# Making the beta-scaled values of the delta rule ahead of its solves

## The chip, the cores and the metric

The kernel runs on one core of one Trainium2 chip. The metric is the device time of one execution in microseconds. Three runs of the kernel before gave 1041.5, 1041.88 and 1042.18 us; the median is 1041.88 us. A further execution was recorded by the profiler, and every duration below comes from it.

## What is computed

One residual encoder block works on 512 tokens of width 1024: a SwiGLU feed-forward half step, a token mixer, and a second feed-forward half step, all in f32. The mixer adds two groups of heads, a gated delta rule (4 heads of width 128) and a latent attention (4 heads). The change lies in the delta rule. Cut to what matters, for each chunk:

```python
A = jnp.where(strict, beta[..., :, None] * kk * decay, 0.0)
M = A + jnp.eye(CHUNK)
rhs = jnp.concatenate([v * beta[..., None], k * (beta * jnp.exp(G))[..., None]], axis=-1)
W = lax.linalg.triangular_solve(M, rhs, left_side=True, lower=True, unit_diagonal=True)
u, wk = W[..., :GDN_DV], W[..., GDN_DV:]
...
v_new = u_c - wk_c @ state
o_c = qd_c @ state + qk_c @ v_new
state = state * gl_c + kd_c.T @ v_new
```

The product `v * beta` (in the kernel with the norm of k folded into the factor) is the subject. It needs the convolved and activated values and one factor per token and head. It does not need the inverse of M.

## The kernel before, in words

The kernel treats the 512 tokens as four blocks of 128. Activations lie with features on the partitions; dense products are split into three matmuls each (lines 453, 454 and 455, high and low parts) so that f32 accuracy comes out.

**Order of emission.** The code is a set of generators. `dense_units` (line 1271) emits one 128-column unit of a projection as four steps of two k-tiles, six matmuls each, and behind each step it advances three side queues by a rate: `chain` (keys, the matrix A, its inverse, then the solves), `deltas` (the products of q and k, the norms of q) and `att` (the attention). The mixer runs the units of k, of q, of v and of z (the output gate) in this order, four units each, which is 16 steps each. During z the rates are 1 for `chain`, 0.75 for `deltas` and 2.67 for `att`. `deltas` runs its generators one after the other: `delta_qk` (4 blocks of work) and `delta_q` (4 and one more), which go in during v and the first steps of z. Behind z a loop (line 2059) advances `chain` by two, the attention by four, and when the attention is through, `out_attended` (line 2108), the attention's part of the output projection. Behind that loop `recur` (line 1702) carries the state from block to block, with its matmuls in the order in which they are written.

**Queues.** The emitted order is not quite the order of the engines' queues. The tile framework fills each engine's queue by a list schedule: of the instructions that its model holds ready, the one emitted first goes first. [...]

**The solve.** `inverse(p)` builds the inverse U of block p through eight stages (lines 1598 to 1668), all four blocks interleaved. `solve(p)` (line 1670), two blocks interleaved, does in its first stage: four transposes of the values into a PSUM bank (`token_major`, line 1489), the product `vb` on VectorE from that bank (helper `mul`, line 1269), for p > 0 the product `kbg`, for p < 3 the product `kd` (both line 1269, from SBUF). In its second stage eight matmul records multiply U with `vb` (line 1689), and ScalarE copies the result `uu` (line 1691). In its third stage, for p > 0, eight records multiply `kbg` with U (line 1698), copied to `w` (line 1700). `recur(0)` begins with line 1730, which needs `uu` and `kd` of block 0.

**Buffers.** Most SBUF tiles of 128x512 f32 come from one pool of 56 slots (`slot`, line 113). The convolved tiles of k, q and v come from another, of 12 (`slot(late=True)`, lines 1477 and 951). PSUM has two pools: three banks for dense products (`pa`) and five for all else (`pb`).

Of the kernel before, what the change touches and what calls it, by code (L numbers as in the profile page):

```python
# [23 lines left out]
NB = NT // P  # L24
# [68 lines left out]
class Block:  # L93
# [1576 lines left out]
    def solve(self, p, vT):  # L1670

        nc = self.nc
        h4 = lambda x: x.rearrange("p (h d) -> p h d", h=4)
        hs = lambda h: slice(h * P, (h + 1) * P)
        c4 = slice(4 * p, 4 * p + 4)
        u = self.inv[p]
        vb = self.slot(s="vb")
        self.mul(h4(vb), h4(self.token_major(vT, p)), self.bc(self.kn[:, c4], 4))
        kt = self.kt[p]
        if p > 0:  # L1680
            kbg = self.slot(s="kbg")
            self.mul(h4(kbg), h4(kt), self.bc(self.eG[:, c4], 4))
        if p < NB - 1:
            self.kd[p] = self.slot(s="kd")
            self.mul(h4(self.kd[p]), h4(kt), self.bc(self.kcd[:, c4], 4))
        yield
        pu = self.aux()
        for h in range(4):
            nc.tensor.matmul(pu[:, hs(h)], u[:, hs(h)], vb[:, hs(h)], start=True, stop=True)
        self.us[p] = self.slot(s="uu")  # L1690
        nc.scalar.copy(self.us[p], pu)
        if p == 0:
            self.wk[0] = True
            return
        yield
        pw = self.aux()
        for h in range(4):
            nc.tensor.matmul(pw[:, hs(h)], kbg[:, hs(h)], u[:, hs(h)], start=True, stop=True)
        self.wk[p] = self.slot(s="w")
        nc.scalar.copy(self.wk[p], pw)  # L1700

    def recur(self, p):

# [264 lines left out]
    def mixer(self, norms):  # L1968
# [21 lines left out]
                self.table(t, t, AF.Silu, after=after)  # L1990

        self.inv = [None] * NB
        self.kd, self.us, self.o, self.wk = ([None] * NB for _ in range(4))
        self.S = None

        def prepared():
# [33 lines left out]
        def solving():  # L2030
            solves = Side(wide=2)
            solves.add(*(self.solve(p, vT) for p in range(NB)))
            while solves.open or solves.todo:
                solves.step(2)
                yield

        chain.add(solving())
        self.dense_units(4, Rates(sides, (1, 0.75, 2.67)), 1, z_done)
        w1 = self.ins["ffn2_w_in"][0]
        self.firsts, early = [], Side()  # L2040
# [164 lines left out]
```

## Time and profile before

| | us |
|---|---|
| median of the runs | 1041.88 |
| lowest and highest run | 1041.5 and 1042.18 |
| the profiled execution | 1041.97 |
| its span in the trace | 1040.3 |
| outside the span | 1.67 |
| VectorE busy | 753.8 |
| ScalarE busy | 498.5 |

In the rows below, a line L1689 is line 1689 of the kernel. PE is the matmul engine (TensorE), PEld its weight loads, DVE is VectorE, ACT is ScalarE, POOL is GpSimd, SP issues the DMAs. A timeline row gives start, duration, engine, line, operation, the tile written and the tiles read (without numbers), shapes and count; in brackets the idle time of that engine just before, and what ended it. Durations of pipelined instructions overlap, so the step from one start to the next is what an instruction costs its engine. A window row gives, for a stretch of the span, its length and the busy time and count of each engine.

### The profile page before, as it was taken

The page shows a single profiled execution, that of the slowest core. Times are in us where ns is not written, and L with a number is a line of the kernel's source. Part 1 is how long each engine was busy: PE and PEld are TensorE (multiplying, and loading weights), DVE is VectorE, ACT ScalarE, POOL GpSimd, SP SyncE. Part 2 cuts the span into 40 slices and gives each one's busy share as a digit, 9 for nine tenths or more (in the row PEclk, how much of TensorE's full clock was granted, in tenths as well). Part 3 has the DMA queues.
Part 4 walks back from the last instruction along what each step waited for, and adds up shares of the span by engine and source line. Part 5 has one row for each costly group of instructions (what it writes and reads, how often), then busy time and mean ns, then how long its engine had stood idle before and what let it go on. Part 6 is the DMA issues. An engine that isn't in the chain of part 4 may idle for free.

```text
span 1040.3 us, 16767 instructions
## 1 busy us (share of the span) xinstructions
PE 1023.9 (98%) x6601; PEld 907.6 (87%) x6601; DVE 753.8 (72%) x1327; ACT 498.5 (48%) x910; POOL 29.6 (3%) x74
## 2 busy tenths in 40 slices
PE   7999999999999999999999989999999999999998
PEld 5788899999887898888788779998999999987888
DVE  5789788887787757868697467787788888783221
ACT  4452455556322235478864454364555555632221
POOL 0000000001000000000000001100000000000000
PEclk9999999999999999999999999999999999999999
DMA  9977234334688744211232031103333334383311
GB/s 330 320 230 255 76 89 122 89 116 130 213 297 280 241 126 130 61 42 41 61 83 65 21 87 36 42 24 96 105 92 112 108 97 121 114 271 105 112 48 42
DMA packets 201501, 130.77 MB, mean 126 GB/s; under 512 B 14017, under 2 KB 186062, under 8 KB 201422
## 3 DMA queue, kind: packets, MB, share of 16 engines
q1 hardware_dynamic: 201422, 129.69, 40.7%
q8 instruction: 52, 0.85, 0.3%
q14 instruction: 27, 0.22, 0.1%
HBM read 127.18 MB, written 2.49 MB: 125 GB/s over the span
## 4 chain that ended last, share of the span: by engine, by line
PE 93%; DVE 3%; issue 1%; DMA 1%; POOL 0%; SPq 0%; ACT 0%; POOLq 0%
PE pa L453 17%; PE pa L454 17%; PE pa L455 17%; PE pa L341 17%; PE pb L341 12%; PE pb L1937 1%; PE pb L453 1%; PE pb L455 1%; PE pb L454 1%; PE pb L1917 1%; DMA ar<-in_w_ada 1%; PE pb L1537 1%; PE pb L632 1%; PE pb L1919 0%; PE pb L1489 0%
## 5 line engine op out<-in xcount | busy, mean ns | idle before, releaser
L223 ACT CAST wh<-wr 128x1024 fp32r<-128x1024 f32 (+1 forms) x104 | 103.6, 1002 | 198.7 <-PE pa L454 174.8
L224 DVE TENSOR_TENSOR wl<-wr,wh 128x1024 fp32r<-128x1024 f32 (+1 forms) x104 | 120.5, 1163 | 80.6 <-ACT wh L223 78.6
L453 PE MATMUL pa<-ah,wh 128*128 128x512 f32 (+1 forms) x396 | 146.5, 370 | 0.0
L454 PE MATMUL pa<-al,wh 128*128 128x512 f32 (+1 forms) x396 | 145.0, 366 | 0.0
L455 PE MATMUL pa<-ah,wl 128*128 128x512 f32 (+1 forms) x396 | 144.9, 366 | 0.0
L257 DVE TENSOR_TENSOR wl<-wr,wh 128x1024 fp32r<-128x1024 f32 x90 | 110.0, 1223 | 44.4 <-ACT wh L261 44.4
L453 PE MATMUL pa<-hh,wh 128*128 128x512 f32 (+1 forms) x357 | 136.9, 384 | 0.0
L454 PE MATMUL pa<-hl,wh 128*128 128x512 f32 (+1 forms) x357 | 135.2, 379 | 0.0
L455 PE MATMUL pa<-hh,wl 128*128 128x512 f32 (+1 forms) x357 | 135.2, 379 | 0.0
L261 ACT CAST wh<-wr 128x1024 fp32r<-128x1024 f32 x90 | 91.8, 1052 | 2.7 <-DMA ar<-in_w_ada 1.8
L453 PEld LDWEIGHTS pa<-ah,wh 128*128 128x128 f32 x396 | 74.7, 189 | 14.5 <-ACT wh L223 2.5
L455 PEld LDWEIGHTS pa<-ah,wl 128*128 128x128 f32 x396 | 74.7, 189 | 12.1
L454 PEld LDWEIGHTS pa<-al,wh 128*128 128x128 f32 x396 | 74.7, 189 | 11.7
L453 PEld LDWEIGHTS pa<-hh,wh 128*128 128x128 f32 x357 | 67.3, 189 | 13.3 <-ACT th L1264 0.8
L813 DVE SCALAR_TENSOR_TENSOR aa<-ar,sc,aa 128x512 f32<-128x512 f32 x98 | 73.3, 749 | 6.3 <-DMA ar<-in_w_ada 4.3
L455 PEld LDWEIGHTS pa<-hh,wl 128*128 128x128 f32 x357 | 67.3, 188 | 11.6
L454 PEld LDWEIGHTS pa<-hl,wh 128*128 128x128 f32 x357 | 67.4, 189 | 10.7
L341 PE MATMUL pa<-hh,wh 128*128 128x256 f32 x240 | 68.0, 283 | 0.0
L341 PE MATMUL pa<-th,wh 128*128 128x256 f32 x240 | 67.9, 283 | 0.0
L341 PE MATMUL pa<-tl,wh 128*128 128x256 f32 x240 | 67.9, 283 | 0.0
L341 PE MATMUL pa<-th,wl 128*128 128x256 f32 x240 | 67.9, 283 | 0.0
L341 PE MATMUL pa<-hl,wh 128*128 128x256 f32 x240 | 67.9, 283 | 0.0
(434 smaller groups left out, 2375.3 us busy)
## 6 DMA issues: line engine op xcount, KB each, us to landing
wr<-in_ffn_w_in SPq DMA_DIRECT2D x79, 512.0 KB, 5.0
ar<-in_w_ada SPq DMA_DIRECT2D x104, 256.0 KB, 5.6
wr<-in_ffn_w_out SPq DMA_DIRECT2D x32, 512.0 KB, 4.2
wr<-in_w_in SPq DMA_DIRECT2D x21, 512.0 KB, 4.3
ar<-in_w_ada SPq DMA_DIRECT2D x20, 512.0 KB, 5.9
wr<-in_ffn_w_out SPq DMA_DIRECT2D x16, 384.0 KB, 4.7
wr<-in_w_out SPq DMA_DIRECT2D x8, 512.0 KB, 3.3
wr<-in_ffn_w_in SPq DMA_DIRECT2D x8, 384.0 KB, 5.9
```

The source lines that it names most:

```text
L223: self.nc.scalar.copy(hi, raw)
L224: self.nc.vector.tensor_tensor(out=lo, in0=raw, in1=hi.bitcast(F32), op=ALU.subtract)
L257: sub = lambda out, x, y: nc.vector.tensor_tensor(out=out, in0=x, in1=y, op=ALU.subtract)
L261: nc.scalar.copy(hi[:, :n], raw[:, :n])
L341: nc.tensor.matmul(z, a[:, j, :], b, start=start and j == 0 and i == 0, stop=j == 3 and i == 2, skip_group_check=not start)
L453: mm(out, wh, xh, start=start, stop=False)
L454: mm(out, wh, xl, start=False, stop=False)
L455: mm(out, wl, xh, start=False, stop=stop)
L632: nc.tensor.matmul(pg[32 * q:32 * q + 32, :256], self.sc[:, kc:kc + 1].to_broadcast([P, 32]), a[kc], start=(e == 0), stop=(e == 1), tile_p ...
L813: nc.vector.scalar_tensor_tensor(out=acc, in0=a, scalar=sc, in1=acc, op0=ALU.mult, op1=ALU.add)
L1537: nc.tensor.matmul(pa[:, ps], kh[:, ps], x[:, ps], start=True, stop=True)
L1917: nc.tensor.matmul(ps[:, :n], self.qnT[h][:, ts], self.knT[h][:, :n], start=True, stop=False)
```

## The change

The product `vb` leaves the solve's first stage and gets a function of its own, `values`, which makes the four transposes and the one multiplication of a block. A generator that calls it for the four blocks is put at the end of the `deltas` queue, ahead of the units of z. The solve uses what it finds, and makes the product itself only if it is not there yet. Nothing else is changed; the number of instructions is the same.

```diff
         u = self.inv[p]
-        vb = self.slot(s="vb")
-        self.mul(h4(vb), h4(self.token_major(vT, p)), self.bc(self.kn[:, c4], 4))
-        kt = self.kt[p]
+        if self.vb[p] is None:
+            self.values(p, vT)
+        vb, kt = self.vb[p], self.kt[p]
         if p > 0:
             kbg = self.slot(s="kbg")
             self.mul(h4(kbg), h4(kt), self.bc(self.eG[:, c4], 4))
...
+    def values(self, p, vT):
+        h4 = lambda x: x.rearrange("p (h d) -> p h d", h=4)
+        self.vb[p] = self.slot(s="vb")
+        self.mul(h4(self.vb[p]), h4(self.token_major(vT, p)), self.bc(self.kn[:, 4 * p:4 * p + 4], 4))
...
-        self.kd, self.us, self.o, self.wk = ([None] * NB for _ in range(4))
+        self.kd, self.us, self.o, self.wk, self.vb = ([None] * NB for _ in range(5))
...
         chain.add(solving())
+
+        def ahead():
+            for p in range(4):
+                self.values(p, vT)
+                yield
+
+        deltas.add(ahead())
         self.dense_units(4, Rates(sides, (1, 0.75, 2.67)), 1, z_done)
```

## The prediction

> **What bounds the kernel now.** I read the page's engine shares first, then the chain that ended last, then busy time in stretches around the change, then the engines' timelines inside the stretch that has idle time.
>
> ```profile
> span 1040.3 us, 16767 instructions
> PE 93%; DVE 3%; issue 1%; DMA 1%; POOL 0%; SPq 0%; ACT 0%; POOLq 0%
> ```
>
> Of the chain that ended last 93% is work of the matmul engine; 3% is VectorE's. Moving matmul work changes nothing; only removing time in which PE stands still does. The windows show where it stands still near the change.
>
> ```profile
> 560.00:580.00 20.00, 19.91 (x173) 16.83 (x171) 13.59 (x29) 9.85 (x28) 2.01 (x2) 1.00 0.00 1
> 580.00:600.00 20.00, 20.00 (x170) 14.25 (x169) 9.00 (x24) 9.25 (x22) 0.00 (x0) 1.00 0.14 42
> 600.00:620.00 20.00, 17.23 (x141) 13.91 (x139) 13.05 (x28) 10.91 (x21) 2.02 (x2) 1.00 0.31 92
> 620.00:640.00 20.00, 19.55 (x143) 18.17 (x144) 15.58 (x27) 10.48 (x23) 3.06 (x3) 1.00 0.10 28
> ```
>
> The first number after the length is PE. From 560 to 600 us PE idles 0.09 us; from 600 to 640 it idles 2.77 + 0.45 = 3.22 us, the hole that the change can work on. What PE does there:
>
> ```profile
> 612.89 0.63 PE L1959 MATMUL pb<-ident,on 128*128 128x128 f32 x4 [0.77 <-DVE on L1269]
> 613.45 0.68 PE L1663 MATMUL pb<-U,Y 64*64 64x64 f32 x8
> 614.05 0.55 PE L1489 MATMUL pb<-ident,cv 128*128 128x128 f32 x3
> 614.35 0.48 PE L453 MATMUL pa<-mh,wh 128*128 128x512 f32 x1
> 614.67 0.71 PE L1489 MATMUL pb<-ident,cv 128*128 128x128 f32 x5
> 615.13 0.48 PE L453 MATMUL pa<-mh,wh 128*128 128x512 f32 x1
> ...
> 616.82 0.39 PE L455 MATMUL pa<-mh,wl 128*128 128x512 f32 x1
> 618.87 2.33 PE L1689 MATMUL pb<-vb,U 128*128 128x128 f32 x16 [1.66 <-DVE vb L1269]
> 621.04 0.60 PE L1489 MATMUL pb<-ident,cv 128*128 128x128 f32 x4
> 621.47 1.06 PE L1698 MATMUL pb<-U,kbg 128*128 128x128 f32 x8
> 622.91 1.16 PE L1689 MATMUL pb<-vb,U 128*128 128x128 f32 x8 [0.38 <-DVE vb L1269]
> 623.91 0.60 PE L1489 MATMUL pb<-ident,cv 128*128 128x128 f32 x4
> 624.35 1.06 PE L1698 MATMUL pb<-U,kbg 128*128 128x128 f32 x8
> 625.29 1.16 PE L1689 MATMUL pb<-vb,U 128*128 128x128 f32 x8
> 626.29 1.06 PE L1698 MATMUL pb<-U,kbg 128*128 128x128 f32 x8
> 627.18 1.06 PE L1730 MATMUL pb<-uu,kd 128*128 128x128 f32 x8
> ```
>
> The inverse ends at 614.05. PE transposes the values, does the nine dense matmuls that lie at hand, and then waits 1.66 us for the first `vb` and 0.38 us for the third: **2.04 us for the product that the change moves.** From 614.05 to 627.18 are 13.13 us, in steps from start to start: transposes 0.30 + 0.46 + 0.43 + 0.44 = 1.63; the nine dense matmuls 0.32 + 2.08 = 2.40; L1689 2.17 + 1.00 + 1.00 = 4.17; L1698 1.06 + 0.94 + 0.89 = 2.89; idle 2.04. The first sixteen of L1689 cost 2.17 where two groups of eight cost 2.00 later on: 0.17 us more, a short pause for the second `vb`.
>
> Why is `vb` late? VectorE's queue:
>
> ```profile
> 614.50 0.73 DVE L1965 SCALAR_TENSOR_TENSOR ml<-pb,cwT,mh 128x512 fp32r<-128x512 f32 x1
> 616.12 1.41 DVE L2119 SCALAR_TENSOR_TENSOR xT<-pa,mod,xT 128x512 f32<-128x512 f32 x2 [0.88 <-PE pa L455]
> 617.44 0.68 DVE L1265 TENSOR_TENSOR fl<-fr,fh 128x512 fp32r<-128x512 f32 x1
> 618.04 0.68 DVE L1269 TENSOR_TENSOR vb<-pb,kn 128x512 f32<-128x512 f32 x1
> 618.64 0.68 DVE L1269 TENSOR_TENSOR kd<-ktk,kcd 128x512 f32<-128x512 f32 x1
> 619.24 0.68 DVE L1269 TENSOR_TENSOR vb<-pb,kn 128x512 f32<-128x512 f32 x1
> 619.84 0.68 DVE L1269 TENSOR_TENSOR kbg<-ktk,eG 128x512 f32<-128x512 f32 x1
> ```
>
> The transposes of blocks 0 and 1 were through at about 615.4, but `vb` of block 0 started at 618.04: ahead of it stand two residual additions (L2119), of which the first waited 0.88 us for dense matmuls, and a weight split `fl`. From 616.1 to 623 the path runs through VectorE.
>
> **The change part by part.** *Removed waits.* With all `vb` made long before, L1689 of blocks 0 and 1 needs only U, which is there. The 2.04 us of idle time and the 0.17 us pause go: 2.21 us. *Moved matmul work.* Sixteen transposes, 1.63 us here, go into a stretch in which PE is full. They cost the same there and are missing here: zero. *Moved VectorE work.* Four multiplications at 0.60 us a step (618.04 to 618.64) are 2.4 us. `deltas` advances 0.75 per step of z; the norms of q take its first four steps' share, so the four calls fall on steps 6, 7, 8 and 10 of the 16. The inverse, of eight stages, goes one stage further in four steps, so these are its second and third stage, ahead of the fourth (L1644, still at work at 588.97 below): my estimate is 570 to 590 us. There VectorE has room:
>
> ```profile
> 578.70 0.69 DVE L1922 TENSOR_REDUCE mx<-pb 128x1 f32<-128x512 f32 x1 [3.10 <-PE pb L1920]
> 588.97 0.28 DVE L1644 TENSOR_SCALAR U<-pb 32x128 f32<-32x128 f32 x1 [2.08 <-PE pb L1642]
> ```
>
> Its cover is these gaps (9.00 of 20 us busy). If the cover fails, each multiplication can hold up one link of the inverse or of the attention by 0.60 us, 2.4 us at most, and nothing is to be won there since PE does not idle; I take 0, nearest to the 9.00, and keep 2.4 for the range. Each call holds one of five `pb` banks from its transposes to its multiplication, with the same bounds. ScalarE, POOL and SP get nothing: the moved step issues neither a copy nor a DMA, and passes no queue of theirs.
>
> *What is late next.* The third stage of block 1 (L1698) needs `kbg`, which stays on VectorE, and so does `kd`. After the change PE goes on at 614.05 with two groups of L1689 (2.00) and nine dense matmuls (2.40) and is free at 618.45. When is `kbg` of block 1 ready? `fl` needs the ScalarE cast of its high part:
>
> ```profile
> 616.09 0.60 ACT L1264 CAST fh<-fr 128x512 fp32r<-128x512 f32 x1
> ```
>
> If VectorE takes `fl` at 616.7, one residual addition (0.7), `kd` (0.6) and `kbg` (0.6 and its end), `kbg` is there at 619.3: a new wait of 0.85 us. If it keeps today's order, the two additions now wait for dense matmuls that come 2.00 us later less the 0.76 us of transposes: 617.35 to 618.65, `fl` to 619.25, `kd` to 619.85, `kbg` to 620.5: a new wait of 2.1 us. If `kd` and `kbg` go ahead of the additions, there is none. I take 0.85 and keep 0 and 2.1.
>
> The queue that decides this is seen in the rows: `kd` reads only `ktk` and `kcd`, which the code makes during the units of q, and yet it stood behind `vb` while VectorE idled 0.88 us. [...]
>
> **Sum.** -2.21 + 0 + 0 + 0.85 = -1.36 us, call it -1.3. The profiled execution took 1041.97 us (span 1040.3 and 1.67 outside it, untouched), 0.09 over the median of 1041.88; against the median the forecast is 1040.6 us.
>
> **Rivals.** *First: the wait only changes its name.* VectorE keeps today's order and PE waits 2.1 us for `kbg` at L1698 instead: 1041.8 us. For it: `kbg` and `kd` stand right behind `vb` in the same queue. Against it: without the transposes nothing but `fl` holds them there.
>
> *Second: full relief.* `kd` and `kbg` come early, -2.21 us, and the solve's matmuls, ready earlier, also fill the waits of 0.77 us (row above) and 0.34 us just before:
>
> ```profile
> 610.92 0.50 PE L454 MATMUL pa<-ml,wh 128*128 128x512 f32 x1 [0.34 <-DVE ml L1965]
> ```
>
> That is up to -3.3 us, 1038.6 to 1039.7 us. For it: block 0's inverse is the first to end. Against it: the solve is emitted behind the whole inverse.
>
> *Third, slower: slots.* The values' tiles lie in the pool of 12, but `vb` comes from the common 56. Counting by the code what is held about 575 us: the input of the mixer 16, k by tokens 4, A 4, qk 4, v of the attention 4, U 4, and of the attention's open heads, z and the mixed output about 12; with four to six short-lived tiles that is 51 to 53. Four `vb` held from there to the solve leave one free, or none. Then the attention's or the inverse's next tile waits for another's release. A sign that slots are scarce already:
>
> ```profile
> SPq L131 <- DVE U L1644: 25.6, 1, 25.6
> ```
>
> SP stood 25.6 us before a load of the next feed-forward's weights into such slots, until the inverse was well on. The price: one link of attention slips behind the end of z's dense matmuls, where little filler is left. Its part off PE is
>
> ```profile
> 580.57 0.15 DVE L1924 TENSOR_TENSOR mx<-mx,rqn 128x1 f32<-128x1 f32 x1
> ...
> 581.84 0.78 ACT L196 ACTIVATE pr<-pb,mx,rqn 128x512 f32<-128x512 f32 x1
> ...
> 587.45 0.59 ACT L1933 COPY pT<-pb 128x512 f32<-128x512 f32 x1 [0.17 <-PE pb L1931]
> ```
>
> with the 0.69 of the reduction above 2.2 us; two of them exposed, one for each of the last two heads, are 4.4 us, and less the 1.3 won +3.1: 1045.0 us. It decides from the point where fewer than four slots are free while z's units run. Against it: no row of 560 to 600 us shows PE, VectorE or ScalarE standing for a slot today, and z's last unit frees the 16 input tiles one by one.
>
> *Fourth: it does not do what it says*, because the multiplications stay queued where they were: 1041.9 us. Little speaks for it, since nothing in the step waits for the inverse.
>
> **How the numbers follow.** A measurement of this kernel tells about 0.2% from no change, 2.1 us: faster is below 1039.8, slower above 1044.0. Forecast 0.35 (1040.0 to 1041.4), first rival 0.10, second 0.26, third 0.26, fourth 0.03. Faster is the second rival, 0.26; slower the third, 0.26; within 0.2% the rest, 0.48. The queues are laid out anew by any change, so the outer cases keep weight. The range goes from the far end of the second, 1038.5, to 1045.2, just beyond the third's price; the unknown 2.4 us of the z stretch on top of the forecast (1043.0) lies inside. The likeliest case alone spans 1040.0 to 1041.4.
>
> **What would show it.** Right: four `vb` multiplications and 16 transposes between 570 and 595 us; no wait for `vb` at L1689; PE's next wait in the solve names `kbg` at L1698 and is near 0.85 us; PE idle from 600 to 640 falls from 3.22 to about 2. First rival: that wait near 2.1. Third: new idle time of PE between 590 and 615 with attention or inverse as the releaser, and ScalarE or VectorE rows there that wait for a tile's earlier reader. The forecast is wrong if PE idles newly in 560 to 600 us, or if the order of the attention's and inverse's matmuls is another.

## The result, and the profile after

The changed kernel took 1040.34 us (median of 21 runs) where the kernel before took 1042.71 us (median of 21 runs). The ratio on record, with its interval, is not quite that of the medians (0.9977): it is **0.9981, 95% interval 0.9975 to 0.9987**, or 2.0 us faster, between 1.35 and 2.6 us. That is just inside the 0.2% that the prediction set as the limit of "no change", and the interval leaves zero out. The forecast was a gain of 1.3 us, just below the interval: taken off the 1041.88 us of the forecast, 2.0 us give 1039.9, between the forecast's likeliest case (1040.0 to 1041.4) and the second rival's (1038.6 to 1039.7). Which of the two it was, the traces tell.

Line numbers behind the solve are 5 higher in the new kernel (L1730 is now L1735, L1715 is L1720, L1964 was L1959), and those behind the new generator 12 higher (L2131 was L2119). First the page of the kernel after, the head and the chain by engine (its trace has one record fewer than the one before, though the diff takes no instruction away):

```profile
span 1038.6 us, 16766 instructions
...
PE 93%; DVE 3%; issue 2%; DMA 1%; SPq 0%; POOL 0%; ACT 0%; POOLq 0%
```

The bound is the same, PE. Then the four windows of the kernel after (length, then busy time of PE, PEld, DVE, ACT, POOL):

```profile
560.00:580.00 20.00, 19.91 (x168) 17.49 (x167) 13.97 (x29) 9.01 (x26) 2.02 (x2) 1.00 0.01 4
580.00:600.00 20.00, 20.00 (x174) 14.29 (x173) 9.66 (x23) 9.03 (x23) 0.00 (x0) 1.00 0.09 27
600.00:620.00 20.00, 18.89 (x158) 15.23 (x156) 12.12 (x28) 10.77 (x22) 2.02 (x2) 1.00 0.36 107
620.00:640.00 20.00, 19.32 (x140) 17.81 (x139) 16.11 (x31) 12.09 (x27) 3.09 (x3) 1.00 0.09 27
```

PE idles 0.09 us between 560 and 600, as before: the moved work made no new hole. Between 600 and 640 it idles 1.11 + 0.68 = 1.79 us instead of 3.22. The PE timeline of the kernel after shows what is left:

```profile
613.01 0.50 PE L454 MATMUL pa<-ml,wh 128*128 128x512 f32 x1 [0.34 <-DVE ml L1970]
...
614.98 0.63 PE L1964 MATMUL pb<-ident,on 128*128 128x128 f32 x4 [0.77 <-DVE on L1269]
615.54 0.67 PE L1663 MATMUL pb<-U,Y 64*64 64x64 f32 x8
616.14 0.71 PE L1689 MATMUL pb<-vb,U 128*128 128x128 f32 x4
616.61 0.47 PE L453 MATMUL pa<-mh,wh 128*128 128x512 f32 x1
...
619.88 0.40 PE L455 MATMUL pa<-mh,wl 128*128 128x512 f32 x1
620.96 1.13 PE L1698 MATMUL pb<-U,kbg 128*128 128x128 f32 x8 [0.68 <-DVE kbg L1269]
621.92 1.06 PE L1689 MATMUL pb<-vb,U 128*128 128x128 f32 x8
...
625.51 1.06 PE L1735 MATMUL pb<-uu,kd 128*128 128x128 f32 x8
```

No L1689 waits for `vb` any more; the waits of 1.66 and 0.38 us are gone. L1689 starts at 616.14, as soon as the inverse (L1663) is through. In their place stands one wait, 0.68 us, at L1698 for `kbg`. The waits of 0.34 and 0.77 us ahead of it are as they were. VectorE's timeline in the kernel after says why `kbg` is late:

```profile
618.26 0.75 DVE L2131 SCALAR_TENSOR_TENSOR xT<-pa,mod,xT 128x512 f32<-128x512 f32 x1 [0.93 <-PE pa L455]
618.92 0.68 DVE L1265 TENSOR_TENSOR fl<-fr,fh 128x512 fp32r<-128x512 f32 x1
619.52 0.69 DVE L1269 TENSOR_TENSOR kd<-ktk,kcd 128x512 f32<-128x512 f32 x1
620.12 0.68 DVE L1269 TENSOR_TENSOR kbg<-ktk,eG 128x512 f32<-128x512 f32 x1
```

One residual addition, the weight split `fl`, one `kd`, then `kbg`: PE waited out the end of this row of four. The second of the two additions, which stood ahead of `fl` in the kernel before, now comes behind `kbg` (at 621.33). The moved work itself stands where it was looked for; the row of the tile `vb` groups the four multiplications, and the first and the last of the four groups of transposes in the PE timeline are

```profile
L1269 DVE TENSOR_TENSOR vb<-pb,kn x4: 651/664/685, 571.5 to 583.0; 128x512 f32<-128x512 f32 x4
```

```profile
569.89 0.60 PE L1489 MATMUL pb<-ident,cv 128*128 128x128 f32 x4
...
579.01 0.60 PE L1489 MATMUL pb<-ident,cv 128*128 128x128 f32 x4
```

**How far the trace agrees with the runs.** Two executions differ in their first 50 us (the last section shows it), so spans are compared here from a common anchor, the first matmul of the inverse:

```profile
550.17 1.16 PE L1618 MATMUL pb<-t,at 128*128 128x128 f32 x8
```

in the kernel before, and in the kernel after

```profile
550.33 1.16 PE L1618 MATMUL pb<-t,at 128*128 128x128 f32 x8
```

From there to the end of the span are 1040.3 - 550.17 = 490.1 us before and 1038.6 - 550.33 = 488.3 after: 1.8 us less, inside the interval of the runs. All of it is won by the end of the solve: from the anchor to the first matmul of the recurrence are 627.18 - 550.17 = 77.01 before and 625.51 - 550.33 = 75.18 after, 1.83 less. From there to the end both take 413.1 us.

### The profile page after: what moved, and what is told of

It reads as the page before. It is cut to its first block, busy times and chain, and to the rows that moved or that the text cites. A ratio compares the mean times of both kernels' runs of the same rounds, so it can differ in the third digit from the quotient of the medians.

```text
span 1038.6 us, 16766 instructions
## 1 busy us (share of the span) xinstructions
PE 1022.6 (98%) x6601; PEld 906.7 (87%) x6601; DVE 752.9 (72%) x1327; ACT 498.3 (48%) x910; POOL 29.7 (3%) x74
## 4 chain that ended last, share of the span: by engine, by line
PE 93%; DVE 3%; issue 2%; DMA 1%; SPq 0%; POOL 0%; ACT 0%; POOLq 0%
PE pa L453 17%; PE pa L454 17%; PE pa L455 17%; PE pa L341 17%; PE pb L341 12%; PE pb L1942 1%; PE pb L453 1%; PE pb L455 1%; PE pb L454 1%; PE pb L1922 1%; DMA ar<-in_w_ada 1%; PE pb L1537 1%; PE pb L632 1%; PE pb L1489 0%; PE pb L1924 0%
## 5 line engine op out<-in xcount | busy, mean ns | idle before, releaser
L341 PE MATMUL pa<-hh,wl 128*128 128x256 f32 x240 | 67.9, 283 | 0.0
```

Of the source, the lines that this page charges most:

```text
L341: nc.tensor.matmul(z, a[:, j, :], b, start=start and j == 0 and i == 0, stop=j == 3 and i == 2, skip_group_check=not start)
```

## The experiments

The theory on trial is the prediction's: PE stood still for `vb`, that wait is gone, and `kbg` with `kd` ahead of it is late next. Its rivals: the gain comes from less VectorE work in the stretch of the solve, whatever is taken out of it; or the held tiles make slots scarce and eat part of the gain. Every kernel is the changed one with an edit. The column "to the end" is the one worked out above, for the profiled execution. From the first matmul of the recurrence to the end it holds 413.1 or 413.2 us in every kernel (e4: 412.7), so what tells the kernels apart lies ahead of that. Five of them (the change, e6, e7, e9, e10) need 9.36 or 9.37 us from the end of the inverse to the recurrence, and still differ by up to 0.4 us in the column; a difference of that size in the column alone is not worth explaining.

| kernel | ratio to before, 95% | to the end |
|---|---|---|
| before | 1 | 490.1 |
| the change | 0.9981 (0.9975 to 0.9987) | 488.3 |
| e1, two `vb` ahead | 0.9983 (0.9972 to 0.9993) | 488.8 |
| e2, `kd` behind `kbg` | 0.9977 (0.9967 to 0.9986) | 487.8 |
| e3, `kbg` and `kd` ahead too | 0.9980 (0.9971 to 0.9989) | 487.8 |
| e4, made right ahead of the solve | 0.9990 (0.9980 to 1.0000) | 488.8 |
| e5, as e3, solve joined to the inverse | 0.9988 (0.9975 to 1.0000) | 487.9 |
| e6, dummy tiles, freed at once | 0.9980 (0.9971 to 0.9990) | 488.3 |
| e7, each `vb` made three times | 0.9986 (0.9975 to 0.9998) | 488.1 |
| e8, only `kbg` and `kd` ahead | 0.9993 (0.9984 to 1.0001) | 489.5 |
| e9, eight slots held | 0.9982 (0.9972 to 0.9992) | 487.9 |
| e10, twelve slots held | 0.9978 (0.9968 to 0.9988) | 488.2 |

Between two of these kernels the intervals of the runs mostly overlap; what tells them apart are the waits in their traces.

### e1: two of the four products ahead

```diff
-            for p in range(4):
+            for p in range(2):
                 self.values(p, vT)
```

> Only blocks 0 and 1 are made ahead; 2 and 3 stay inside their solves. Theory of waits (the gain is PE's idle time for vb in the solve, given back in part as a new wait for kbg): the 1.66 us wait is gone; the transposes of blocks 2 and 3 are back in the solve and serve PE as filler while kbg of block 1 is made (0.44 us each), so PE idles 0.3 to 0.5 us there in all and the time is 2.0 to 2.4 us under the kernel before, as good as the full change. Rival of load (the gain is VectorE work taken out of the solve, 0.6 us a block): half the change's gain, 1.0 us under the kernel before.

The PE timeline of e1:

```profile
618.75 1.13 PE L1698 MATMUL pb<-U,kbg 128*128 128x128 f32 x8 [0.24 <-DVE kbg L1269]
620.52 1.16 PE L1689 MATMUL pb<-vb,U 128*128 128x128 f32 x8 [0.64 <-DVE vb L1269]
...
623.46 1.16 PE L1689 MATMUL pb<-vb,U 128*128 128x128 f32 x8 [0.45 <-DVE vb L1269]
```

The wait of 1.66 us is gone, as expected. But with blocks 2 and 3 made in the solve again, waits for `vb` come back there, 1.09 us, and with the 0.24 left of the wait for `kbg` PE idles 1.33 us where 0.3 to 0.5 were expected. The gain from the anchor, 1.3 us (490.1 to 488.8), lies between the 2.0 to 2.4 of the theory and the 1.0 of the rival, so this kernel does not decide between them; by the runs it can't be told from the change. Most of the change's 1.8 us belongs to the first two blocks; the 0.5 of the other two is little more than the column can tell.

### e2: kd behind kbg

```diff
-        if p < NB - 1:
-            self.kd[p] = self.slot(s="kd")
-            self.mul(h4(self.kd[p]), h4(kt), self.bc(self.kcd[:, c4], 4))
         yield
...
         nc.scalar.copy(self.us[p], pu)
+        if p < NB - 1:
+            self.kd[p] = self.slot(s="kd")
+            self.mul(h4(self.kd[p]), h4(kt), self.bc(self.kcd[:, c4], 4))
```

> The changed kernel with the kd product emitted behind the copy of uu, so that kbg of block 1 is the first product of the solve in VectorE's queue; no work is taken out. Theory of waits: the 0.68 us wait of PE for kbg at its eight matmuls shrinks by one multiplication, 0.60 us, to about 0.1 us, and the time is 2.6 us under the kernel before. Rival of load: VectorE has as much to do there as in the changed kernel, so 2.0 us under the kernel before, like the change.

The DVE and the PE timeline of e2:

```profile
619.64 0.68 DVE L1265 TENSOR_TENSOR fl<-fr,fh 128x512 fp32r<-128x512 f32 x1
620.24 0.68 DVE L1269 TENSOR_TENSOR kbg<-ktk,eG 128x512 f32<-128x512 f32 x1
620.84 1.28 DVE L1269 TENSOR_TENSOR kd<-ktk,kcd 128x512 f32<-128x512 f32 x2
```

```profile
621.07 1.13 PE L1698 MATMUL pb<-U,kbg 128*128 128x128 f32 x8
```

No work was taken from VectorE, only the order of its products changed (`kbg` ahead of `kd`), and the wait of 0.68 us is gone: L1698 has no bracket, PE idles 0.08 us in all from 620 to 640, and the kernel ends 0.5 us earlier from the anchor. All of that lies in the solve: from the end of the inverse to the recurrence it takes 8.84 us instead of 9.37. So the new wait is one of order in VectorE's queue: `kbg` starts 0.60 us after `fl` here (619.64 to 620.24) and 1.20 us after it in the change (618.92 to 620.12), where `kd` stands between the two.

### e3: kbg and kd ahead as well

```diff
         self.mul(h4(self.vb[p]), h4(self.token_major(vT, p)), self.bc(self.kn[:, 4 * p:4 * p + 4], 4))
+        c4, kt = slice(4 * p, 4 * p + 4), self.kt[p]
+        if p > 0:
+            self.kbg[p] = self.slot(s="kbg")
+            self.mul(h4(self.kbg[p]), h4(kt), self.bc(self.eG[:, c4], 4))
+        if p < NB - 1:
+            self.kd[p] = self.slot(s="kd")
+            self.mul(h4(self.kd[p]), h4(kt), self.bc(self.kcd[:, c4], 4))
```

The solve uses what it finds; its own lines for `kbg` and `kd` are taken out.

> The changed kernel with kbg and kd of all blocks made ahead too, in the same calls as vb: six more multiplications (3.6 us of VectorE) and six more tiles of the common 56 leave the solve for the units of z. Theory of waits: the 0.68 us wait for kbg goes and nothing else, 2.7 us under the kernel before. Rival of load: 3.6 us more off VectorE's queue in the solve is worth another 1.5 to 3 us, 3.5 to 5 us under the kernel before. Rival of slots (prediction's third): ten tiles held instead of four leave no free slot, PE idles newly between 575 and 615 us, and the time is at or above that of the kernel before.

Two windows of e3, and the one new wait in its PE timeline:

```profile
580.00:600.00 20.00, 19.53 (x188) 14.48 (x187) 10.10 (x27) 9.72 (x26) 1.39 (x1) 1.00 0.35 108
...
620.00:640.00 20.00, 20.00 (x146) 18.62 (x145) 13.39 (x24) 13.45 (x29) 3.09 (x3) 1.00 0.09 27
```

```profile
594.25 0.43 PE L1642 MATMUL pb<-U,Y 32*32 32x32 f32 x8 [0.41 <-DVE U L1644]
```

Nothing in the solve waits now, and PE idles nowhere from 620 to 640. Six more multiplications, 3.6 us of VectorE, left the solve's stretch. From the end of the inverse to the recurrence that saves 0.93 us (8.44 instead of 9.37), the wait of 0.68 us and some pace; ahead of it the kernel is 0.41 us slower, with 0.47 us of new idle time, 0.41 of it at the inverse's fourth stage. It ends where e2 ends, 2.4 us under the kernel before from the anchor, and the 3.5 to 5 us of the rival of load do not come. The work removed is not what counts.

### e4: made right ahead of the solve

```diff
-        chain.add(solving())
-
         def ahead():
...
-        deltas.add(ahead())
+        chain.add(ahead(), solving())
```

> The changed kernel with the same four calls put directly ahead of the solves in the chain's queue, not in the units of z: vb is a step of its own, but made when the inverse is through. Theory of waits: vb stands behind the residual additions and the weight split in VectorE's queue again, and kbg behind four vb; PE idles 1.5 to 2.5 us there, and the time is within 0.7 us of the kernel before. Rival of place (any step ahead of the solve will do, since all four are made without the kd and kbg between them): 1 to 2 us under the kernel before.

The PE timeline of e4:

```profile
619.07 0.55 PE L1489 MATMUL pb<-ident,cv 128*128 128x128 f32 x3
...
623.13 2.05 PE L1689 MATMUL pb<-vb,U 128*128 128x128 f32 x16 [0.47 <-DVE vb L1269]
626.21 1.13 PE L1698 MATMUL pb<-U,kbg 128*128 128x128 f32 x8 [1.03 <-DVE kbg L1269]
```

All transposes stand ahead of the solve and fill PE, yet PE waits 0.47 + 1.03 = 1.50 us, against 2.04 before and 0.68 after. The kernel won 1.3 us from the anchor where the change won 1.8; by the runs it won 1.0 us, between 0 and 2.1. PE's idle time is what the theory expected (1.5 to 2.5), the gain is not: it is past the theory's 0.7 and in the rival's 1 to 2. Any step of its own ahead of the solve already helps; the early place is worth the rest.

### e5: each solve joined to its own inverse

```diff
+        def joined(p):
+            yield from self.inverse(p)
+            yield from self.solve(p, vT)
...
-            inv.add(*(self.inverse(p) for p in range(NB)))
+            inv.add(*(joined(p) for p in range(NB)))
```

on top of e3, with `solving` left out.

> All products ahead (as in the run with kbg and kd ahead too), and each block's solve emitted right behind its own inverse instead of behind all four. Theory of waits: the solve's matmuls of the first blocks are ready while PE waits 0.34 us and 0.78 us for the attention's last head (between 610 and 618 us), and fill these waits: 1.1 us less than with all products ahead, 3.5 us under the kernel before. Rival: the order of the PSUM banks and the copies behind the solve keep the matmuls where they are; same as with all products ahead, 2.1 to 2.4 us under the kernel before.

The PE timeline of e5:

```profile
614.10 0.50 PE L454 MATMUL pa<-ml,wh 128*128 128x512 f32 x1 [0.34 <-DVE ml L1972]
...
616.07 0.63 PE L1966 MATMUL pb<-ident,on 128*128 128x128 f32 x4 [0.77 <-DVE on L1269]
616.62 0.68 PE L1663 MATMUL pb<-U,Y 64*64 64x64 f32 x8
617.23 1.16 PE L1684 MATMUL pb<-vb,U 128*128 128x128 f32 x8
```

The waits of 0.34 and 0.77 us stand as before and no solve matmul got ahead of the last L1663. The gain from the anchor is 2.2 us, as the rival here said, and not 3.5. The full relief of the prediction's second rival, -3.3 us, is not to be had in this way: the four inverses end together.

### e6, e9 and e10: are slots scarce?

e6 gave each `vb` two dummy tiles, set by POOL in `values` and again by POOL in the solve, which was to release them.

```diff
         yield
+        for t in self.held[2 * p:2 * p + 2]:
+            nc.gpsimd.memset(t[:, :1], 0.0)
         pu = self.aux()
...
+        self.held = [self.slot(s="hold") for _ in range(2)] + (self.held if p else [])
+        for t in self.held[:2]:
+            self.nc.gpsimd.memset(t[:, :1], 0.0)
```

> The changed kernel with eight more tiles of the common 56 held, two per call of values, from the units of z until the solve of the block; nothing is computed in them (one column is set to zero by POOL). Theory of waits: within 0.4 us of the changed kernel, 1.6 to 2.3 us under the kernel before, since PE had z's matmuls and the inverse to go on with. Rival of slots: twelve held tiles leave none for the attention's and the inverse's short-lived ones; PE idles newly between 575 and 615 us, and the time is 1 to 4 us above the changed kernel.

It cost nothing, but it proves nothing: in its rows of the dummy tile the second setting follows the first within a microsecond, so nothing was held until the solve.

```profile
L1710 POOL MEMSET hold<- x8: 99/99/101, 570.6 to 583.3; 128x1 f32 x8
L1688 POOL MEMSET hold<- x8: 99/99/100, 571.2 to 583.5; 128x1 f32 x8
```

So the release was tied to the solve's own product (e9; in e10 two tiles each):

```diff
         nc.scalar.copy(self.us[p], pu)
+        for t in self.held[1 * p:1 * p + 1]:
+            nc.scalar.copy(t[:, :4], pu[:, :4])
...
+        self.held = ([] if p == 0 else self.held) + [self.slot(s="hold") for _ in range(1)]
+        for t in self.held[1 * p:]:
+            self.nc.gpsimd.memset(t[:, :4], 0.0)
```

> The changed kernel, and each call of values() also takes one slot of the pool of 56, set by a small POOL memset and released only by a small ScalarE copy out of the first product of the solve, right behind the uu copy: with the four vb, eight slots are held from the z stretch to the solve. Theory of the waits (slots are not short): within 0.4 us of the changed kernel from the first L1618 to the end of the span (488.3), PE idle in 560 to 600 us below 0.3; the small copies of ScalarE may cost up to 0.3 in the solve. Rival of the slots: by the count of 51 to 53 slots in use, eight held ones are three to five too many, so tiles of the attention or the inverse wait for a release, PE idles newly between 575 and 615 us, and the kernel loses 1.5 to 3.1 us against the changed one.

> As the one before with two more slots for each vb: twelve slots are held from the z stretch to the solve. Theory of the waits: within 0.5 us of the changed kernel from the first L1618 to the end of the span, since the kernel with vb, kbg and kd ahead held ten without a loss. Rival of the slots: dearer than with eight held, +2 to +5 us, with PE idle between 575 and 615 us and rows there whose releaser is the reader of an older tile; if only this kernel and not the one with eight pays, the point from which slots decide lies between eight and twelve.

The rows of the dummy tile in e10, and two of its windows:

```profile
L1710 POOL MEMSET hold<- x8: 101/101/102, 572.2 to 587.0; 128x4 f32 x8
L1693 ACT COPY hold<-pb x8: 160/186/212, 622.9 to 627.9; 128x4 f32<-128x4 f32 x8
```

```profile
560.00:580.00 20.00, 19.92 (x153) 17.70 (x152) 15.02 (x29) 9.02 (x21) 1.61 (x7) 1.00 0.08 25
580.00:600.00 20.00, 20.00 (x191) 14.94 (x190) 9.53 (x26) 10.12 (x28) 1.21 (x3) 1.00 0.27 83
```

Now the tiles are held, set from 572 to 587 us and released from 623 to 628, twelve slots with the four `vb`, and PE is as full between 560 and 600 as without them; both kernels end within 0.4 us of the change. The rival of the slots falls, up to twelve held. The forecast's count of 51 to 53 slots in use would have left room for five at most, so it was too high by seven or more, or what waits for a slot there delays nobody; these rows do not tell which.

### e7: is VectorE's spare time the cover?

```diff
-        self.mul(h4(self.vb[p]), h4(self.token_major(vT, p)), self.bc(self.kn[:, 4 * p:4 * p + 4], 4))
+        pt = self.token_major(vT, p)
+        for _ in range(3):
+            self.mul(h4(self.vb[p]), h4(pt), self.bc(self.kn[:, 4 * p:4 * p + 4], 4))
```

Each product is made three times, the same values each time.

> The changed kernel with each vb multiplication done three times over from the same PSUM bank: 8 more multiplications, 4.8 us of VectorE in the units of z. Theory of cover (VectorE is half idle there, PE is full): within 0.4 us of the changed kernel, 1.6 to 2.3 us under the kernel before. If the cover fails, each multiplication holds up a link of the inverse or the attention by 0.6 us: up to 4.8 us above the changed kernel, PE idle newly between 565 and 600 us.

Two windows of e7:

```profile
580.00:600.00 20.00, 19.22 (x181) 13.90 (x179) 10.90 (x26) 9.29 (x25) 0.00 (x0) 1.00 0.42 128
600.00:620.00 20.00, 18.20 (x154) 14.51 (x154) 12.76 (x28) 11.85 (x23) 2.02 (x2) 1.00 0.02 6
```

Eight more multiplications, 8 x 0.60 = 4.8 us on VectorE. PE idles 0.78 us from 580 to 600, the first sign of the cover wearing thin, and yet the kernel ends no later from the anchor (488.1). From the anchor to the end of the inverse it takes 65.59 us against 65.81 in the change, so the 0.78 was given back in the pace of the matmuls; no row says where. The cost of 0 that the forecast took for 2.4 us of VectorE work holds.

### e8: the other products ahead, vb where it was

```diff
-        if self.vb[p] is None:
-            self.values(p, vT)
-        vb, kt = self.vb[p], self.kt[p]
+        vb = self.slot(s="vb")
+        self.mul(h4(vb), h4(self.token_major(vT, p)), self.bc(self.kn[:, 4 * p:4 * p + 4], 4))
...
-        self.vb[p] = self.slot(s="vb")
-        self.mul(h4(self.vb[p]), h4(self.token_major(vT, p)), self.bc(self.kn[:, 4 * p:4 * p + 4], 4))
```

`vb` is made inside the solve again, and only `kbg` and `kd` go ahead as in e3.

> The kernel before with vb left in the solve and the six kbg and kd multiplications made ahead instead: 3.6 us of VectorE leave the solve against 2.4 us in the change. Theory of waits: the first vb stands behind the residual additions and the weight split as before, so the 1.66 us wait stays; the 0.38 us wait and the 0.17 us pause go: 0.4 to 0.7 us under the kernel before. Rival of load: 3 us under the kernel before.

The PE and the DVE timeline of e8:

```profile
619.00 2.02 PE L1683 MATMUL pb<-vb,U 128*128 128x128 f32 x16 [1.66 <-DVE vb L1269]
```

```profile
616.24 1.41 DVE L2130 SCALAR_TENSOR_TENSOR xT<-pa,mod,xT 128x512 f32<-128x512 f32 x2 [0.89 <-PE pa L455]
617.57 0.68 DVE L1265 TENSOR_TENSOR fl<-fr,fh 128x512 fp32r<-128x512 f32 x1
618.17 1.28 DVE L1269 TENSOR_TENSOR vb<-pb,kn 128x512 f32<-128x512 f32 x2
```

3.6 us of VectorE work left the stretch, more than the 2.4 that the change takes out, and the gain is 0.6 us from the anchor (by the runs 0.7, not clear of zero). The wait of 1.66 us for the first `vb` stands unchanged, since what delays it are the additions and `fl` ahead of it. The second and third `vb` come sooner, and that is the 0.6. The rival of the mere load, which asked for 3 us here, falls with this kernel, e2 and e3.

## Why the prediction was right, point by point

**Removed waits (2.21 us): right.** No L1689 waits for `vb`, and the pause within the first sixteen is gone. e8 shows that it is this product that did it.

**Moved transposes (0): right within 0.1.** In the solve's stretch they cost 1.63 us. In the stretch of z the steps from start to start of the four groups are 0.44, 0.44, 0.50 and 0.35, together 1.73.

**Moved VectorE work (0, bound 2.4): right.** No new idle time from 560 to 600 us, and e7 put three times as much there.

**What is late next (0.85, bounds 0 and 2.1): right in kind, 0.68 in size, the size in part by luck.** The four instructions ahead of PE's wait were the ones taken, but not in the order taken. The forecast let VectorE begin with `fl`, as soon as its cast was through, and put the addition behind it; in the trace the addition runs first, from 618.26, before that cast is through (it starts at 618.18 on ScalarE and takes 0.60), and `fl`, `kd`, `kbg` follow without a gap. So, counted from the end of the inverse, L1698 could start on `kbg` after 4.82 us (forecast 5.25). PE was free sooner too, after 4.14 us (forecast 4.40), and the two misses leave a wait that is only 0.17 us off.

**The sum (-1.36): short by 0.5 in the trace.** The mis-sized term is what the solve's matmul groups cost once nothing interrupts them. From the end of the inverse to the recurrence the forecast had 13.13 - 2.99 = 10.14 us, and the trace has 625.51 - 616.14 = 9.37. Of these 0.77 us, 0.17 are the smaller wait. 0.26 lie in the stretch with sixteen records of L1689 and nine dense matmuls, 4.14 instead of 4.40: the sixteen, now mixed with dense matmuls, took 1.64 and not two times 1.00, the nine 2.50 and not 2.40. 0.34 lie in the five groups from L1698 on, 4.55 instead of 4.89: the forecast carried over steps of 0.94 to 1.06 from groups that had come behind a wait, behind transposes or, at 625.29, just as their `vb` came (VectorE's row of it starts at 624.54 and takes 0.69), but in an unbroken row they step by 0.89 to 0.90, with 0.96 for the first, which follows the wait. Against this stand 0.30 us more between the anchor and the end of the inverse than the transposes explain by their old price; 0.10 of it is their own new price. The other 0.20 lie ahead of L1942 at 594.30 (L1937 at 592.22 before); from there to the end of the inverse the two kernels differ by 0.01. In sum 0.77 - 0.30 = 0.47 beyond the forecast: 1.83.

**The rivals.** That the wait only changes its name was half true: there is a new wait for `kbg`, a third of the old one and not all of it. Full relief did not come by itself. Its first part is to be had by order alone (e2), some 0.5 us; the waits of 0.34 and 0.77 did not yield (e5). Slots did not decide anything up to twelve held. And the change did what it says. One sign that the prediction gave for being wrong did come up in part: the inverse's and the attention's matmuls are in another order for a while. In the kernel before, eight of the inverse (L1634, 578.09) stand between two lines of one attention step (L1919 at 577.77 and L1920 at 578.46); in the kernel after they stand behind that step (L1634 at 581.46, behind L1925 at 581.00). From the 594.30 named above on, their order is the old one. PE has no new idle time there, and beside the transposes that stretch lost no more than the 0.20 us above.

The sign that the prediction saw for the slots did not hold. SP's wait of 25.6 us for a reader of U has no row in the kernel after, though four more tiles are held. Instead the first row of SP's waits has grown by 25.0 us and one wait; in the kernel before and then in the kernel after it reads

```profile
SPq L131 <- DVE wl L224: 335.9, 75, 22.9
```

```profile
SPq L131 <- DVE wl L224: 360.9, 76, 24.1
```

SP, it seems, stands as long as before and only for another tile.

**The best version** seen is e2 or e3, 0.5 us ahead of the change from the anchor. By the runs alone it can't be told from the change.

## What to carry to other kernels

Look at what stands ahead of a late operand in its engine's queue, not at how busy that engine is: 2.4 us of VectorE work were worth 1.8 us here because they had stood behind work that itself waited for PE, while 3.6 us of other VectorE work from the same stretch were worth 0.6. When a wait is taken away, read off the queue what comes next, and price it; here the swap of two instructions took away the next wait too. And take the price of a matmul group from a row without a wait or another kind of matmul ahead of it, because such neighbours are in the step: here 0.94 to 1.06 us behind them, 0.89 to 0.90 in an unbroken row.

## What the runs showed of the hardware

**The first 50 us differ from execution to execution.** With the same code ahead of the anchor, it lay between 549.5 and 553.8 us. The sixth group of L632 starts at 44.90 us in the kernel before, at 45.14 in the kernel after, at 47.09 in e3 and at 48.96 in e4, and from it to the anchor the four take 504.8 to 505.3 us, so in these nearly all of the difference is made ahead of it. These are the first window and the first group of L632 in the kernel before, then the same two rows in e4, whose anchor came last:

```profile
0.00:50.00 50.00, 43.03 (x269) 32.14 (x270) 30.88 (x68) 22.21 (x37) 2.35 (x12) 1.00 0.98 335
```

```profile
12.33 1.09 PE L632 MATMUL pb<-ar,sc 128*32 128x256 f32 x16 [1.16 <-DMA ar<-in_w_ada]
```

```profile
0.00:50.00 50.00, 42.51 (x250) 30.23 (x250) 27.12 (x60) 20.38 (x34) 2.35 (x12) 0.90 0.93 318
```

```profile
12.85 1.96 PE L632 MATMUL pb<-ar,sc 128*32 128x256 f32 x16 [2.36 <-DMA ar<-in_w_ada]
```

In e4 PE had stood 2.36 us, and the same sixteen matmuls took 1.96 us instead of 1.09; the granted clock of the window is 0.90, where the kernel before has 1.00. The next group of L632 in e4, at 22.28 us, took 1.12 us again. Three of the twelve executions (e3, e4, e10) show the 1.96, all behind 2.29 to 2.37 us of idle time, and their anchors are the latest three, 551.7 to 553.8. But e6 had stood 2.36 us as well and took 1.09, at a granted clock of 1.00, so the length of that wait alone does not decide; what does stays open. A difference of 1 us between two spans of this kernel says nothing until both are counted from a common instruction.
